# A hybrid encoder layer on one core: each recurrent head's four weight tiles as two units of seven products of block sums

## The chip, the cores and the metric

The kernel runs on one core of a Trainium2 chip. The metric is the time of one execution on the device in microseconds (us); three executions of the kernel before took 2068.74, 2071.32 and 2077.0 us, median 2071.32.

## The reference, cut to what matters

One layer over 1056 tokens (1024 of a prompt, 32 of a sample): a fused input projection, window attention (branch A), a gated linear recurrence (branch B), gates, an output projection and a convolutional FFN. The change is in branch B and in how its columns of the projection are multiplied:

```
h = _rms_norm(x, g_pre_mix);  z = h @ w_in            # 1024 x 7424 weights
qb, fb, ib, ob = the columns of z for branch B         # 8 heads x 128 columns each
f = lb + (1 - lb) * sigmoid(fb);  k = 1 - f;  q = silu(qb);  v = ib
cum = cumsum(log f) in blocks of 64 tokens
o = (q * exp(cum)) @ state + causal(q * exp(cum - mid) @ (k * exp(mid - cum)).T) @ v
state = exp(last) * state + (k * exp(last - cum)).T @ v
yb = rms_norm(o) * silu(ob)
```

All of it is float32. TensorE gets every operand as two parts, a rounded one (hi) and the rest (lo), so one product of a 128x128 weight block is three matmuls: hi x hi, hi x lo, lo x hi.

## The kernel before, in words

Tokens lie along the free axis in three column groups, `GR` (384, 384 and 288 wide; the last holds 256 prompt tokens and the sample). `La[g][k]` and `Lb[g][k]` are the hi and lo parts of h for row block k of group g; they stay in SBUF from the first stage until branch B is done. A weight tile is 1024x128, loaded by `load_raw`, split by `load_next` (ACT rounds, L174; DVE takes the rest, L177) and used as a `unit` of three blocks, one per group; a block is 24 matmuls (8 row blocks x 3, L193 to L195) into one PSUM bank of three (`mm`), in two halves of 12. `stream` runs the blocks and hangs small pieces of work behind each half.

The order of the stages: norm and transposes of x; attention, with the gate columns and q columns as filler (up to 390 us); the eight heads of branch B (390 to 890 us); four gate units (GB[4..7]); the products with w_br_a, w_br_b and w_out; the FFN's up projection (1240 to 1695 us, `up_unit`), which already multiplies by block sums; the down projection and the end.

A head of branch B is four units in the order i, og, f, q. `decay` (L723) takes the logarithm of f and scans it, `factors` (L733) makes the exponentials of a group, `k_turn` and `v_turn` transpose, `tile_in` (L797) and `tile_out` (L837) carry the recurrence over nine token tiles with the PSUM banks `s` (two) and `o` (one), `group_out` (L865) transposes a group of normalised outputs and gates them. A head's recurrence runs behind the units of the next head, one tile per two halves. Each engine executes its instructions in the order that the scheduler wrote down; where one waits, all behind it on that engine wait.

## Time and profile before

| What | Value |
|---|---|
| median of three runs | 2071.32 us |
| the profiled execution | 2065.69 us, its span 2064.0 us |
| TensorE busy | 2021.0 us (98%) |
| VectorE (DVE) busy | 1339.9 us (65%) |
| ScalarE (ACT) busy | 895.1 us (43%) |
| GpSimd (POOL) busy | 187.2 us (9%) |
| TensorE's granted clock in the head stage | 1.00 of full |

Busy is the union of an engine's instructions. Matmuls are pipelined: one starts before the one ahead of it has ended, so what a matmul costs TensorE is the step from its start to the next start, not its duration. The same holds in a small way on DVE and ACT.

### The profile page before, as it was taken

What the parts mean: (1) busy time and instruction counts of PE and PEld (TensorE: products, weight loads), DVE (VectorE), ACT (ScalarE), POOL (GpSimd) and SP (SyncE); (2) the same over time, 40 slices, a digit from 0 to 9 for tenths busy, and PEclk for the clock granted to TensorE, in tenths of its full rate; (3) what the DMA queues carried; (4) which work ended last, traced back from release to release, by engine and by line L of the source; (5) the groups of instructions that cost most, each with busy time, mean ns of one, the idle gap of its engine ahead of it and who ended that gap; (6) DMA issues with size and microseconds to landing.
All of it is one profiled execution on the core that took longest, in us unless ns stands there. A gap on an engine that the chain in (4) does not pass through costs nothing.

```text
span 2064.0 us, 37303 instructions
## 1 busy us (share of the span) xinstructions
PE 2021.0 (98%) x14474; PEld 1993.4 (97%) x14474; DVE 1339.9 (65%) x3070; ACT 895.1 (43%) x1984; POOL 187.2 (9%) x244
## 2 busy tenths in 40 slices
PE   7999999999999999999999989999999999999998
PEld 6999999999999999999999988999999999999998
DVE  6776778446665556654354678888888884655552
ACT  6554555444444444442123664333333344543432
POOL 1000000000000000000000012323333310000000
PEclk9999999999999999999999999999999999999999
DMA  7312221211111111267554463222222245654542
GB/s 228 104 60 76 79 65 62 70 42 56 43 42 54 55 41 56 64 200 236 164 177 126 130 196 99 71 94 70 86 73 83 73 137 189 222 179 168 166 132 81
DMA packets 253574, 224.34 MB, mean 109 GB/s; under 512 B 12421, under 2 KB 229016, under 8 KB 253397
## 3 DMA queue, kind: packets, MB, share of 16 engines
q1 hardware_dynamic: 251893, 217.48, 33.5%
q0 software_dynamic: 1504, 4.47, 0.7%
q8 instruction: 114, 1.87, 0.4%
q14 instruction: 63, 0.52, 0.1%
HBM read 167.07 MB, written 54.83 MB: 108 GB/s over the span
## 4 chain that ended last, share of the span: by engine, by line
PE 82%; DVE 8%; DMA 5%; ACT 2%; issue 2%; SPq 0%; POOL 0%; ACTq 0%; DVEq 0%; POOLq 0%
PE mm L193 18%; PE mm L195 17%; PE mm L194 17%; PE st L1284 6%; PE st L1282 6%; PE st L1283 6%; PE tr L450 1%; DVE wl L177 1%; PE s L816 1%; PE o L472 1%; DVE cb L731 1%; PE s L423 1%; DMA ac<-act_d 1%; PE o L473 1%; PE s L424 1%
## 5 line engine op out<-in xcount | busy, mean ns | idle before, releaser
L193 PE MATMUL mm<-La,wh 128*128 128x384 f32 (+1 forms) x1368 | 459.1, 336 | 0.0
L194 PE MATMUL mm<-Lb,wh 128*128 128x384 f32 (+1 forms) x1368 | 440.5, 322 | 0.0
L195 PE MATMUL mm<-La,wl 128*128 128x384 f32 (+1 forms) x1368 | 440.2, 322 | 0.0
L1282 PE MATMUL st<-op,wt 128*128 128x264 f32 x1232 | 349.4, 284 | 6.0 <-ACT Sp L1293 2.8
L1284 PE MATMUL st<-op,wt 128*128 128x264 f32 x1232 | 350.2, 284 | 0.0
L1283 PE MATMUL st<-op,wt 128*128 128x264 f32 x1232 | 348.2, 283 | 0.0
L177 DVE TENSOR_TENSOR wl<-wr,wh 128x1024 fp32r<-128x1024 f32 x166 | 202.9, 1222 | 163.5 <-ACT wh L174 156.3
L174 ACT CAST wh<-wr 128x1024 fp32r<-128x1024 f32 x145 | 152.0, 1049 | 266.7 <-PE mm L194 215.9
L193 PEld LDWEIGHTS mm<-La,wh 128*128 128x128 f32 x1368 | 257.3, 188 | 2.3 <-issue 1.6
L194 PEld LDWEIGHTS mm<-Lb,wh 128*128 128x128 f32 x1368 | 257.8, 188 | 0.0
L195 PEld LDWEIGHTS mm<-La,wl 128*128 128x128 f32 x1368 | 257.2, 188 | 0.0
L1282 PEld LDWEIGHTS st<-op,wt 128*128 128x128 f32 x1232 | 231.9, 188 | 7.2 <-ACT Sp L1293 3.0
L1283 PEld LDWEIGHTS st<-op,wt 128*128 128x128 f32 x1232 | 232.1, 188 | 0.0
L1284 PEld LDWEIGHTS st<-op,wt 128*128 128x128 f32 x1232 | 231.3, 188 | 0.1
L193 PE MATMUL mm<-ac,wh 128*128 128x352 f32 x528 | 170.8, 323 | 1.3 <-DVE Sp L1311 1.3
L195 PE MATMUL mm<-ac,wl 128*128 128x352 f32 x528 | 170.1, 322 | 0.0
L194 PE MATMUL mm<-ac,wh 128*128 128x352 f32 x528 | 169.5, 321 | 0.0
L1179 ACT CAST wt<-wu 128x512 fp32r<-128x512 f32 x132 | 81.5, 620 | 198.9 <-POOL ab L1268 99.8
L193 PE MATMUL mm<-Ra,wh 128*128 128x264 f32 x512 | 146.5, 286 | 4.7 <-DVE ta L955 3.4
L194 PE MATMUL mm<-Rb,wh 128*128 128x264 f32 x512 | 145.8, 285 | 0.0
L195 PE MATMUL mm<-Ra,wl 128*128 128x264 f32 x512 | 145.7, 285 | 0.0
L1180 DVE TENSOR_TENSOR wt<-wu,wt 128x512 fp32r<-128x512 f32 x132 | 108.3, 820 | 44.2 <-ACT wt L1179 44.0
(349 smaller groups left out, 4146.3 us busy)
## 6 DMA issues: line engine op xcount, KB each, us to landing
wr<-in_w_down_dram SPq DMA_DIRECT2D x66, 512.0 KB
wr<-in_w_in_dram SPq DMA_DIRECT2D x58, 512.0 KB
wu<-in_w_up_dram SPq DMA_DIRECT2D x44, 512.0 KB
act_d<-Up SPq DMA_DIRECT2D x22, 528.0 KB
ac<-act_d SPq DMA_DIRECT2D x66, 176.0 KB
wr<-in_w_out_dram SPq DMA_DIRECT2D x16, 512.0 KB
ya_d<-ya SPq DMA_DIRECT2D x8, 528.0 KB
ld<-ya_d SPq DMA_DIRECT2D x32, 132.0 KB
```

What stands on the lines that cost most here:

```text
L174: S.copy(hi[:], raw[:])
L177: V.tensor_tensor(lo[:], raw[:], hi[:].bitcast(F32), op=ALU.subtract)
L193: E.matmul(ps, wh, a, start=first and n == 0, stop=False)
L194: E.matmul(ps, wh, b, start=False, stop=False)
L195: E.matmul(ps, wl, a, start=False, stop=last and n == len(ks) - 1)
L423: E.matmul(o, q[:, c:c + P], K1[kv][:, k0:k0 + nk], start=True, stop=False)
L424: E.matmul(o, q[:, c:c + P], K2[kv][:, k0:k0 + nk], start=False, stop=True)
L1179: S.copy(t[:, 0], src)
L1180: V.tensor_tensor(t[:, 1], src, t[:, 0].bitcast(F32), op=ALU.subtract)
L1282: E.matmul(o, wh, xh, start=first and k == 0, stop=False, skip_group_check=True)
L1283: E.matmul(o, wh, xl, start=False, stop=False, skip_group_check=True)
L1284: E.matmul(o, wl, xh, start=False, stop=k == 3, skip_group_check=True)
```

## The change

For each head the tiles q and f form one unit, i and og another (`BU`). With the four 512-row quarters a11, a12 (of the first tile) and a21, a22 (of the second) and four blocks of h (rows 0 to 3 and 4 to 7 of groups 0 and 1), a unit computes the two output tiles for groups 0 and 1 from seven products of sums instead of eight products; group 2 is multiplied plainly, with the quarters a11, a12, a21 and a22, which are operands 0, 2, 5 and 6 of the eight that a unit prepares. A product is 12 matmuls, a "piece"; a unit is 11 pieces: 7 of 384 columns into the PSUM banks X, Y and Z, and 4 of 288 into G. The sums of h are made once: its float32 form goes to DRAM (`h_d`), GpSimd adds there in four steps during attention (`h_sums`), and the parts `TH`, `TL` are loaded before the heads. The sums of the weights are made on GpSimd per unit (`b_parts`), and ACT and DVE split eight operands of 512 columns per unit. Evictions (e0 to e10) combine the banks. The block La[1][0:4], Lb[1][0:4] is given up to hold `tf` and `cb` and is read back for the gate units (`back`). Further: the gate unit GB[3] runs alone between attention and the heads; the sums for the norm are taken for six tiles at a time and the scaling (`S.mul`) is on ACT; the affine map of f moves from DVE to ACT; the scan is in three parts; the PSUM bank `s` is single; the recurrence follows at one tile per one and a half pieces.

```diff
-    for h in range(8):
-        plan += [in_cols(c + h * P) for c in (3328, 4352, 2304, 1280)]
+    plan.append(GB[3])
+    n_first = len(plan)
     plan += GB[4:]
...
+        def h_sums(k):
+            top, low = (aq.tile([P, 768], F32, tag=f"hs{a}", name=nm("hs")) for a in range(2))
+            dma(top[:], h_d[:, k, :])
+            dma(low[:], h_d[:, k + 4, :])
+            b11, b12, b21, b22 = top[:, 0:384], top[:, 384:768], low[:, 0:384], low[:, 384:768]
+            G.tensor_tensor(b11, b11, b12, op=ALU.subtract)
+            G.tensor_tensor(b12, b12, b22, op=ALU.subtract)
+            G.tensor_tensor(b22, b22, b11, op=ALU.add)
+            G.tensor_tensor(b21, b21, b22, op=ALU.subtract)
+            for j, b in enumerate((b22, b12, b11, b21)):
+                dma(t_d[j][:, k, :], b)
...
+    SX = {0: (La[0][0:4], Lb[0][0:4]), 1: (rows4(TH[0]), rows4(TL[0])),
+          2: (La[0][4:8], Lb[0][4:8]), 3: (rows4(TH[1]), rows4(TL[1])),
+          4: (rows4(TH[2]), rows4(TL[2])), 6: (rows4(TH[3]), rows4(TL[3])),
+          7: (La[1][4:8], Lb[1][4:8])}
+    BU = []
+    for h in range(8):
+        BU += [(1280 + h * P, 2304 + h * P), (3328 + h * P, 4352 + h * P)]
...
+        def parts(src):
+            t = wp.tile([P, 2, 4, P], F32R, tag="wb", name=nm("wt"), bufs=8)
+            S.copy(t[:, 0], src)
+            V.tensor_tensor(t[:, 1], src, t[:, 0].bitcast(F32), op=ALU.subtract)
+            ready_b.append(t)
+        parts(a11)
+        G.tensor_tensor(s1, a21, a22, op=ALU.add)
+        G.tensor_tensor(s3, a11, a21, op=ALU.add)
+        G.tensor_tensor(a11, a11, s1, op=ALU.add)
+        yield
+        parts(a11)
+        yield
+        parts(a12)
+        G.tensor_tensor(a12, a12, a11, op=ALU.add)
+        yield
+        for src in (s3, s1, a21, a22, a12):
+            parts(src)
+            yield
...
     def s_bank():
-        return bank(pp, "s", 2)
+        return bank(pb, "s", 1)
...
+            return [(st("X", 0, True), e0), (g1a, None), (st("Y", 1, True), e2),
+                    (st("X", 2), lambda: f1(0, b("X"))), (cl("G", 2), lambda: f1(2, b("G", 288))),
+                    (st("Y", 3), e5), (st("Z", 4, True), e6), (g2a, None), (st("Y", 6), e8),
+                    (cl("G", 6), lambda: f2(2, b("G", 288))), (st("Z", 7), e10)]
...
-            V.tensor_scalar(tf[:], tf[:], mc1[:, h:h + 1], c1[:, h:h + 1], op0=ALU.mult, op1=ALU.add)
-            V.tensor_tensor_scan(cb[:], resets[:], bb[:], 0.0, op0=ALU.mult, op1=ALU.add)
+            for o, n in GR:
+                V.tensor_tensor_scan(cb[:, o:o + n], resets[:, :n], cb[:, o:o + n], 0.0,
+                                     op0=ALU.mult, op1=ALU.add)
+            S.activation(tf[:], tf[:], AF.Identity, scale=mc1[:, h:h + 1], bias=c1[:, h:h + 1])
...
+                    S.mul(os_, os_, rs[:m_, a:a + 1])
...
+            pieces += qf_unit(h) + io_unit(h)
+            at(m0 + 11, decay, h)
+            for g in range(3):
+                at(m0 + 12 + 3 * g, factors, h, g)
+            at(m0 + 14, k_turn, h, 0)
...
+            at(m1, v_turn, h, 1)
...
+                t_in = m1 + 1 + (j * 5 // 4 if last else j * 3 // 2)
```

In the order of a middle head, first TensorE where a group of outputs is transposed (`tr` is the transposes' bank, `ident` the identity, `mm` a block's bank). Before:

```order
L194 MATMUL mm_7202<-Lb_165,wh_6826 128x288
L195 MATMUL mm_7202<-La_159,wl_6827 128x288
L871 MATMUL tr_7265<-ident,os_6965 128x128 x3
L193 MATMUL mm_7278<-La_157,wh_6948 128x384
L194 MATMUL mm_7278<-Lb_160,wh_6948 128x384
```

Now, in the fourth piece of the i/og unit (`X` and `G` are its banks, `wt` a split operand, L1063 the outputs' transposes, L981 `k_turn`):

```order
L1063 MATMUL tr_7434<-ident,vk_7036 128x128
L815 MATMUL X_7334<-Lb_169,wt_7279 128x384
L1063 MATMUL tr_7434<-ident,vk_7036 128x128
L816 MATMUL X_7334<-La_163,wt_7279 128x384
L1063 MATMUL tr_7434<-ident,vk_7036 128x128
L981 MATMUL tr_7473<-ident,ke_7395 128x128 x3
L813 MATMUL G_7367<-La_167,wt_7279 128x288
```

The transposes of two groups, which wait for the scaling on ACT, now stand between the matmuls of one piece, and `k_turn` of the current head follows at once; before, one group stood between two blocks.

ScalarE, at the og tanh (`sg`) of a head. Before (`os` are outputs, L719 `v_turn`):

```order
L854 COPY os_6965<-o_6968 128x128
L856 ACTIVATE sq_6971,ss_6966<-os_6965 128x128
L693 ACTIVATE sg_6856<-mm_6952 128x384
L719 COPY vk_6855<-tr_6995 128x256
L721 COPY vk_6855<-tr_6995 32x128
```

Now (`wu` is a raw weight tile that GpSimd has added into, `rs` the norm's factors):

```order
L911 COPY vk_7552<-tr_7553 128x384
L733 CAST wt_7640<-wu_7416 128x512
L898 ACTIVATE sg_7575<-x_1323_7550 128x384
L955 ACTIVATE qx_7612<-d_1335_7610 128x2x128
L957 ACTIVATE qx_7612<-d_1335_7610 128x32
L733 CAST wt_7675<-wu_7416 128x512
L1055 ACTIVATE vk_6959<-vk_6959,rs_7499 128x128 x2
```

The cast of the second operand of the next unit, which needs GpSimd's sum, now stands ahead of the tanh, of a group's exponentials and of the scaling of the outputs.

VectorE, after the factors of a head's first group. Before:

```order
L782 SCALAR_TENSOR_TENSOR tq_6858<-tq_6858,cb_7260 128x384
L813 TENSOR_TENSOR am_7365<-s_7363,cmask 32x32
L828 SCALAR_TENSOR_TENSOR S_7368<-S_7361,dec_6602,s_7363 128x128
L707 SCALAR_TENSOR_TENSOR tq_6858<-tq_6858,mm_7342 128x384
L756 TENSOR_TENSOR qx_7387<-cb_7260 128x3x64
```

Now (L834 is the eviction e2, L1064 the gating of a group of outputs):

```order
L973 SCALAR_TENSOR_TENSOR tq_7108<-tq_7108,cb 128x384
L734 TENSOR_TENSOR wt_7413<-sa_7202,wt_7413 128x512
L834 TENSOR_TENSOR vt_7432<-s1c_7350,Y_7412 128x384
L1064 SCALAR_TENSOR_TENSOR sg_6983<-tr_7380,ghh,sg_6983 128x384
L1004 TENSOR_TENSOR am_7450<-s_7448,cmask 32x32
L1019 SCALAR_TENSOR_TENSOR S_7453<-S_7446,dec_6687,s_7448 128x128
L1064 SCALAR_TENSOR_TENSOR sg_6901<-tr_7434,ghh,sg_6901 128x384
L734 TENSOR_TENSOR wt_7456<-wu_7069,wt_7456 128x512
L943 TENSOR_TENSOR cb<-cb 128x3x64
```

Between two groups' factors now stand the splits of operands, an eviction and the gating of two groups.

## Rows read from the trace of the kernel before

**Rows 1.** The page: busy time of each engine; GB/s moved in 40 slices.
```profile
PE 2021.0 (98%) x14474; PEld 1993.4 (97%) x14474; DVE 1339.9 (65%) x3070; ACT 895.1 (43%) x1984; POOL 187.2 (9%) x244
...
GB/s 228 104 60 76 79 65 62 70 42 56 43 42 54 55 41 56 64 200 236 164 177 126 130 196 99 71 94 70 86 73 83 73 137 189 222 179 168 166 132 81
```
**Rows 2.** Windows: attention, one head, one unit of the up projection.
```profile
core 0: us, PE busy (x) PEld busy (x) DVE busy (x) ACT busy (x) POOL busy (x), PEclk, DMA share, GB/s
...
300.00:320.00 20.00, 20.00 (x142) 19.59 (x141) 17.95 (x53) 12.22 (x36) 1.83 (x10) 1.00 0.17 52
...
603.30:661.70 58.40, 58.06 (x383) 56.80 (x382) 35.63 (x121) 26.64 (x71) 0.00 (x0) 1.00 0.15 45
...
1371.00:1391.30 20.30, 20.30 (x170) 20.30 (x170) 16.65 (x25) 6.99 (x10) 7.02 (x5) 1.00 0.25 78
```
**Rows 3.** Waits in 428.1:836.9: who for whom, us in total, times, longest.
```profile
DVE am L818 <- PE s L816: 119.1, 42, 4.0
...
PEld o L851 <- ACT tq L706: 3.3, 6, 0.6
PE o L851 <- DVE am L813: 2.1, 6, 0.3
```
**Rows 4.** The tile tf: the logarithm of each head.
```profile
L729 ACT ACTIVATE bb<-tf,c,c x8: 1268/1268/1271, 428.1 to 836.9; 128x1056 f32<-128x1056 f32 x8
```
**Rows 5.** Timeline of PE in a head: start, us, line, tile, shape.
```profile
490.62 0.29 PE L193 MATMUL mm<-La,wh 128*128 128x288 f32 x1
...
491.81 0.29 PE L193 MATMUL mm<-La,wh 128*128 128x288 f32 x1
...
498.00 0.33 PE L193 MATMUL mm<-La,wh 128*128 128x384 f32 x1
...
500.08 0.33 PE L193 MATMUL mm<-La,wh 128*128 128x384 f32 x1
```
**Rows 6.** Timeline of DVE in a head.
```profile
543.20 0.83 DVE L730 TENSOR_SCALAR tf<-tf,mc,c 128x1056 f32<-128x1056 f32 x1
543.95 2.35 DVE L731 TENSOR_TENSOR_SCAN cb<-resets,bb 128x1056 f32<-128x1056 bf16 x1
...
550.01 0.55 DVE L777 TENSOR_TENSOR d<-d,tf 128x384 f32<-128x384 f32 x1
550.48 0.55 DVE L778 TENSOR_TENSOR ke<-ke,tf 128x384 f32<-128x384 f32 x1
...
560.30 0.60 DVE L873 SCALAR_TENSOR_TENSOR yb<-tr,ghh,sg 128x384 f32<-128x384 f32 x1
560.83 1.20 DVE L177 TENSOR_TENSOR wl<-wr,wh 128x1024 fp32r<-128x1024 f32 x1
565.83 0.28 DVE L818 TENSOR_TENSOR am<-s,cmask 64x128 int32<-64x128 int32 x1 [3.80 <-PE s L816]
...
566.45 0.29 DVE L826 COPY S<-s 128x128 f32<-128x128 f32 x1
...
585.87 0.67 DVE L861 TENSOR_SCALAR os<-os,rs 128x128 f32<-128x128 f32 x3
```
**Rows 7.** Timeline of DVE in a unit of the up projection.
```profile
1383.73 1.45 DVE L1180 TENSOR_TENSOR wt<-wu,wt 128x512 fp32r<-128x512 f32 x1
...
1388.33 0.69 DVE L1180 TENSOR_TENSOR wt<-wu,wt 128x512 fp32r<-128x512 f32 x1
1388.94 1.25 DVE L1260 TENSOR_TENSOR Up<-Up,rbT 128x1056 f32<-128x1056 f32 x1
```
**Rows 8.** Timeline of POOL in the same unit.
```profile
1374.51 2.20 POOL L1186 TENSOR_TENSOR wu<-wu,wu 128x512 f32<-128x512 f32 x1
...
1383.34 1.29 POOL L1192 TENSOR_TENSOR wu<-wu 128x512 f32<-128x512 f32 x1 [4.33 <-DVE wt L1180]
```
**Rows 9.** Waits of ACT in 1300:1560 (12.8 units of the up projection).
```profile
ACT wt L1179 <- POOL ab L1268: 59.1, 12, 5.0
```
**Rows 10.** Groups of instructions by form: ACT's casts of the up projection.
```profile
L1179 ACT CAST wt<-wu 128x512 fp32r<-128x512 f32 x132 | 81.5, 620 | 198.9 <-POOL ab L1268 99.8 <-PE st L1284 67.6 <-DVE wt L1180 22.6
```

More of the change, by code (lines that the diff above doesn't have):

```diff
@@ L112, in layer_kernel @@
     xt_d = dp.tile([P, 8, T], F32, name="xt_d")
+    h_d = dp.tile([P, 8, 768], F32, name="h_d")
+    t_d = [dp.tile([P, 4, 384], F32, name=f"t_d{j}") for j in range(4)]
     x1_d = dp.tile([P, 8, T], F32, name="x1_d")
@@ L643, in layer_kernel @@
             blocks += unit(gate_out(ta_d[i]))
-            if i in (0, 2, 4, 7):
-                blocks += unit(gate_out(tb_d[(0, 2, 4, 7).index(i)]))
+            if i in GB_AT:
+                blocks += unit(gate_out(tb_d[GB_AT.index(i)]))
             if i < 7:
@@ L662, in layer_kernel @@
         hi_on[0] = "act"
+    bctx = ExitStack()
+    tp = bctx.enter_context(right("tp"))
+    TH, TL = [], []
+    for j in range(4):
+        TH.append(tp.tile([P, 4, 384], F32R, name=f"TH{j}"))
+        TL.append(tp.tile([P, 4, 384], F32R, name=f"TL{j}"))
+        dma(TL[j][:].bitcast(F32), t_d[j][:])
+        for k in (0, 2):
+            src = TL[j][:, k:k + 2, :].bitcast(F32)
+            S.copy(TH[j][:, k:k + 2, :], src)
+            V.tensor_tensor(TL[j][:, k:k + 2, :], src, TH[j][:, k:k + 2, :].bitcast(F32),
+                            op=ALU.subtract)
@@ new lines, in layer_kernel, with b_raw, b_parts @@
+    NB = len(BU)
+    raw_b, ready_b, gens_b, n_b = {}, [], {}, [0]
+    def b_raw(u):
+        raw_b[u] = []
+        for c in BU[u]:
+            t = wp.tile([P, KT, P], F32, tag="wb" if u % 2 else "wr", name=nm("wu"),
+                        bufs=8 if u % 2 else 2)
+            dma(t[:], in_cols(c)[0])
+            raw_b[u].append(t)
+    def b_parts(u):
+        f1, f2 = raw_b.pop(u)
+        ss = wp.tile([P, KT, P], F32, tag="wb", name=nm("sa"), bufs=8)
+        s1, s3 = ss[:, 0:4, :], ss[:, 4:8, :]
+        a11, a12, a21, a22 = f1[:, 0:4, :], f1[:, 4:8, :], f2[:, 0:4, :], f2[:, 4:8, :]
+        def parts(src):
[16 more added lines that the diff above has]
+            yield
@@ new lines, in b_prepare @@
+    def b_prepare(n):
+        while n_b[0] < min(n + 1, 8 * NB):
+            u, i = divmod(n_b[0], 8)
+            if i == 0:
+                if u not in raw_b:
+                    b_raw(u)
+                gens_b[u] = b_parts(u)
+            next(gens_b[u])
+            if i == 4 and u + 1 < NB:
+                b_raw(u + 1)
+            n_b[0] += 1
+    small = {0: [lambda: b_prepare(0)], 2: [lambda: b_prepare(1)], 4: [lambda: b_prepare(2)]}
+    stream(unit(gate_out(tb_d[3])), small)
+    pctx.close()
@@ L665, in layer_kernel, with mm_bank, tr_bank, s_bank @@
+    pctx = ExitStack()
+    pb = pctx.enter_context(tc.tile_pool(name="pb", bufs=1, space=PSUM, reuse_waits="tile"))
+    n_bank = [0]
+    def mm_bank():
+        n_bank[0] += 1
+        return bank(pb, "XYZG"[n_bank[0] % 4], 1)
+    def tr_bank():
+        return bank(pb, "tr", 2)
+    def s_bank():
+        return bank(pb, "s", 1)
+    def o_bank():
+        return bank(pb, "o", 1)
     with right("bp") as bp:
@@ L896, in layer_kernel @@
-        tail = [b for c in range(4, 8) for b in unit(gate_out(tb_d[c]))]
-        stream(blocks + tail[:8], small)
+                at(m0 + 12 + 3 * g, factors, h, g)
+            at(m0 + 14, k_turn, h, 0)
+            at(m0 + 17, k_turn, h, 1)
+            at(m0 + 16, v_turn, h, 0)
+            at(m0 + 18, v_turn, h, 2)
+            at(m1, v_turn, h, 1)
+            last = h == 7
+            for j in range(9):
+                t_in = m1 + 1 + (j * 5 // 4 if last else j * 3 // 2)
+                at(t_in, tile_in, h, j)
+                at(t_in + 2, tile_out, h, j)
+                if j == 2:
+                    at(t_in + 1, k_turn, h, 2)
+                if j == 5:
+                    at(t_in + 4, group_out, h, 0)
+                    at(t_in + 5, group_out, h, 1)
+                if j == 8:
+                    at(t_in + (3 if last else 4), group_out, h, 2)
@@ new lines, in back, with more @@
+        def back():
+            for part, t in (("La", La), ("Lb", Lb)):
+                t[1][0:4] = rows4(lp.tile([P, 4, 384], F32R, tag=f"{part}10", name=nm(part)))
+            for k in range(4):
+                src = Lb[1][k].bitcast(F32)
+                dma(src, h_d[:, k, 384:768])
+            for k in range(4):
+                split(La[1][k], Lb[1][k], Lb[1][k].bitcast(F32))
+        def more():
+            limit[0] = n_mix
+            load_next()
+        at(len(pieces) - 3, back)
@@ L900, in layer_kernel @@
+        at(len(pieces) - 2, more)
+        for m, (run, ev) in enumerate(pieces):
+            run()
+            if ev is not None:
+                ev()
+            for f in small.pop(m, ()):
+                f()
+        tail = []
+        for c in range(4, 8):
+            u = unit(gate_out(tb_d[c]))
+            tail += [u[0], u[2], u[1]]
+        stream(tail[:8], {m - len(pieces): f for m, f in small.items()})
+    bctx.close()
     rp = ctx.enter_context(right("rp"))
```

245 lines of the change are left out of this document (142 added, 103 removed).

## The prediction, made before the changed kernel ran

> **What bounds the kernel now.** I read the page first, then windows over the stages, then who waits for whom in the heads, then timelines of TensorE and DVE inside one head and inside one unit of the up projection, which already works with block sums. TensorE is busy for 98% of the span, so time goes where TensorE's work goes [rows 1]. Inside the heads it stands still for almost nothing: of 58.40 us in a middle head it is busy 58.06, and in seven heads its waits for DVE and ACT sum to 2.1 and 3.3 us [rows 2, 3]. DVE has room there on average, 35.6 of 58.4 us, and most of its idle time is a wait for TensorE's scores; ACT has 26.6, GpSimd nothing [rows 2, 3]. The logarithms of the first and the last head start 408.8 us apart, so a head is 408.8 / 7 = 58.40 us [rows 4].
>
> **What the change removes on TensorE.** Twelve steps of matmuls of 384 columns took 500.08 - 498.00 = 2.08 us, 0.173 each; nine of 288 columns took 1.19 us, 0.132 each [rows 5]. A head before has 4 tiles x 2 groups x 24 = 192 of the first and 96 of the second: 33.3 + 12.7 = 46.0 us. The other 12.4 us of the 58.4 are the recurrence's matmuls and the transposes, which stay. After it has 2 units x 7 pieces x 12 = 168 and 96: 29.1 + 12.7 = 41.8. So TensorE needs 54.2 us per head, 4.16 less, and 33.3 us less over eight heads. The granted clock is full in the head's window [rows 2] and TensorE stays dense, so I leave it there.
>
> **What it adds on DVE and ACT, in total.** Per head DVE gets 16 splits of 512 columns at a step of 0.61 us (1388.33 to 1388.94) [rows 7] for four of 1024 at 1.20 [rows 6]: +5.0. Ten combinations of banks come in, of 384 columns like the product at 550.01, which steps by 0.47 [rows 6]: +4.7. The affine map of f goes (0.75), the scaling of the outputs (0.67 per three, 2.0) and one of three rounds of small norm instructions (about 1) [rows 6]. That is 41.5 us of 54.2 before any quarrel with GpSimd, 77%. ACT gets 16 casts of 0.62 [rows 10] for four of about 1.05, the map, the nine scalings and two copies: about 36 us, 67%. On average both fit; a unit of the up projection has DVE at 16.65 of 20.3 us, 82%, and TensorE waits for nothing [rows 2].
>
> **Where the work stands.** It doesn't lie evenly. All of the scan and the three groups' factors fall into the i/og half of a head, after `decay`. Before, that stretch of DVE ran without a gap from 543.20 to 562.03, 18.8 us [rows 6], and nothing on TensorE waited behind it, since blocks have three banks and the transposes of k come a unit later. Now take out of it the map (0.75), the scaling (0.6), two combinations of q (0.94) and a 1024-wide split (1.2): 15.3 remain. Add eight splits (4.9), five evictions (2.35), three combinations of og (1.3), the gating of two more groups (1.1, at 0.53 a step), a round of small instructions (0.9) and one more tile's mask and state (565.83 to 566.74, 0.9) [rows 6, 7]: 26.8 us. TensorE's own work in that half is 7 x 2.08 + 4 x 1.58 + 6.2 of the small = 27.1.
>
> To that comes GpSimd, which makes four sums of 512 columns per unit. In the up projection one split took 1.45 us instead of 0.69 while a sum ran beside it; the sum ran from 1383.34 to 1384.63, and the split ended 0.55 after it [rows 7, 8]. Another sum took 2.20 instead of 1.29 [rows 8]: the loss falls on either engine. Per unit the loss on DVE lies between 0 (GpSimd always waits) and 4 x 1.29 = 5.2. I take 2.5, half. DVE's half is then 29.3 us against 27.1, and it decides by 2.2 us.
>
> The Trainium skill (SBUF — State Buffer, section "Who interferes with whom") says that a DVE instruction with two SBUF inputs and a GpSimd instruction that reads SBUF lock each other out, and that the later one is blocked until the first has finished. The split above agrees: it finished one undisturbed run's length after the sum. By that rule alone, with DVE always the later one, the loss would be the upper end, 5.2 us; that is the third case below.
>
> Why 2.2 us on DVE become a wait of TensorE: the pieces use single banks. Y is written in pieces 2, 5 and 8 of a unit, and between them only two pieces (3.7 to 4.2 us) cover the eviction, which stands in DVE's queue behind factors and splits, as the order shows. At the half's end `v_turn` of group 1 waits for eviction e10, and e10 stands behind everything else of the half. In the other half DVE has 41.5 + 5 - 29.3 = 17.2 us for TensorE's 27, catches up and hides nothing more. **Waits through ACT** come on top. In the up projection ACT stood 59.1 us in 12 waits, 4.9 each, at a cast that needs GpSimd's sum [rows 9]; nothing was late there, for only casts stand behind it. Here the tanh of og, a group's exponentials and the scaling of the outputs stand behind that cast, and TensorE's transposes of the outputs, now between the matmuls of a piece, wait for the scaling. Between 0 (the sum is early) and 4.9 I take 0.8, near the lower end, as DVE is late at the same place and the two waits mostly fall together. So 54.2 + 2.2 + 0.8 = 57.2 us per head, 1.2 less than before, 9.6 over eight.
>
> **Edges.** In attention GpSimd makes 16 sums of 384 columns, about 1 us each by width, 0 to 16 us on a DVE that is busy 17.95 of 20 us at the densest [rows 2]; little of it is late, as the early windows are thinner: 1. The sums' parts are 4 x 786 KB to load when attention's tiles come free. The unit GB[3] (48 x 0.173 + 24 x 0.132 = 11.5 us) and two pieces (3.7) cover the first; at some 200 GB/s, as the dense slices move [rows 1], all four take 15.7: 0 to 5, I take 1. In the last head the four splits of the gate weights (1.20 each) and of the reloaded block stand in DVE's queue ahead of the first tile's mask, the reload starts only when `cb` is done, and the single bank s holds TensorE: 0 to 8, I take 4. The stores of h and the scan in three parts I count at nothing: the first lie on a queue that nobody waits for, the second costs two start-ups. Edges: 6, between 0 and 15.
>
> **The sum.** Against the profiled execution's 2065.69 us: -9.6 + 6 = -3.6, 2062.1. The median of the runs shown is 5.6 above that execution, so as a median 2067.7: 2068.
>
> **The rivals.**
> *The waits are absorbed (faster).* DVE is at about 80%, as in the up projection where TensorE never waits with three banks and the same eviction chain [rows 2]. If DVE's lead from the light half carries it through, a head is 54.2 to 54.8: -33.3 + 6 = -27, 2044. Against it: in the up projection DVE's load is the same in every unit; here one half is full.
> *DVE and GpSimd bind the second half (slower).* DVE is always the later one: 26.8 + 5.2 = 32.0 us, and ACT's wait at the cast adds 1.5 that DVE spends idle: 33.5 against 27.1. The head is then 60.6, +2.2, and 17.6 + 6 = +24: 2095. It decides from the point where DVE's half exceeds TensorE's by more than the 4.16 us saved. For it: the split of 1.45 us and the 59.1 us of ACT [rows 7, 9]; against it the sum of 2.20, where GpSimd lost [rows 8].
> *The edges are dear.* The heads as forecast, but the edges cost 18: +8, 2080. Against it: attention shows hardly a wait of TensorE now.
> That fewer matmuls are issued is sure from the order; that they would not shorten TensorE's work would need a longer step between the pieces, and the rows on both sides of a change of bank keep their step [rows 5], so I give that no case of its own.
>
> **How the numbers follow.** What a measurement of this kernel tells from no change is about 0.5%, 10 us. Forecast 0.40, with a head of 56.4 to 58.0 and edges of 3 to 9: 2058 to 2077; a quarter of it (0.10) is faster by over 0.5%, 0.05 slower, 0.25 within. Absorbed 0.27, all faster. DVE and GpSimd 0.25, all slower. Dear edges 0.08, 0.02 within and 0.06 slower. Faster 0.37, within 0.27, slower 0.36. The range reaches through most of the second and third case: 2040 to 2097, with about 0.07 left out on either side.
>
> **What would show it.** In the trace after, the step of the matmuls stays at 0.173 us and a head has 264 of them. The distance of the logarithms is the test: 57.2 forecast, 54.5 if absorbed, 60.6 if bound. In the i/og half DVE should show hardly a gap, some splits of about 1.4 us, and TensorE should wait there at `v_turn` of group 1, at Y's pieces and at the outputs' transposes, in the q/f half for almost nothing. Wrong would be: waits of TensorE in the q/f half, casts that are late (a piece waiting for its weights), a wait of more than 8 us at the start of the heads, or attention longer than now.

## The result and the profile after

The changed kernel took 2082.39 us (median of five runs, 2077.66 to 2083.61), the kernel before 2070.11 (median of five); the ratio is 1.005 with a 95% interval of 1.0028 to 1.0072. The forecast was 2068 within 2040 to 2097: it named a small gain or no change, and the change costs half a per cent. The profiled execution took 2079.95 us, its span 2078.2.

The page's busy times, the answer to [rows 1]:

```profile
PE 2011.2 (97%) x14282; PEld 1971.7 (95%) x14282; DVE 1430.1 (69%) x3096; ACT 966.0 (46%) x2182; POOL 290.6 (14%) x323
```

TensorE has 192 matmuls fewer and is busy 9.8 us less, but the span is 14.2 us longer, so it stands still more. Where, is read from three kinds of rows: the last scores of attention, the logarithms of the heads, and the first product of the gated branches behind the heads. First the kernel before, then after (source view; the numbers behind the durations are the first and the last start):

```profile
L423 PE MATMUL s<-K,qa x72: 222/284/388, 70.1 to 370.9; 128*128 128x256 f32 x56, 128*128 128x128 f32 x8, 128*128 128x160 f32 x8
L193 PE MATMUL mm<-Ra,wh x512: 279/282/422, 909.8 to 1201.0; 128*128 128x264 f32 x171
```
```profile
L423 PE MATMUL s<-K,qa x72: 222/306/390, 77.5 to 369.6; 128*128 128x256 f32 x56, 128*128 128x128 f32 x8, 128*128 128x160 f32 x8
L193 PE MATMUL mm<-Ra,wh x512: 281/282/422, 926.8 to 1215.6; 128*128 128x264 f32 x171
L918 ACT ACTIVATE cb<-tf,c,c x8: 1268/1269/1272, 422.2 to 836.5; 128x1056 f32<-128x1056 f32 x8
```

One gate unit fewer lies ahead of attention's last scores: GB[3], 11.5 us by the steps of [rows 5], has moved to between attention and the heads. Without it, the start with attention went from 359.4 to 369.6 (+10.2). From there to the branches it went, GB[3] on both sides, from 550.4 to 557.2 (+6.8). The rest went from 1154.2 to 1151.4 (-2.8). The sum is 14.2. The logarithms are (836.5 - 422.2) / 7 = 59.19 us apart, against 58.40 [rows 4]. Both are means over seven distances, and in both the first is shorter, since no recurrence runs behind the units of head 0: before it is 54.33 and the other six 59.05 to 59.10; after it is 53.79 and the others 59.69 to 59.96, once 61.19 (starts of the logarithms in ACT's timeline, the first three of which follow). So a head behind the first grew by 1.0 us in the mean of six (59.08 to 60.08), although TensorE has by the forecast 4.16 us less to do in it.

```profile
422.23 1.27 ACT L918 ACTIVATE cb<-tf,c,c 128x1056 f32<-128x1056 f32 x1
...
476.02 1.27 ACT L918 ACTIVATE cb<-tf,c,c 128x1056 f32<-128x1056 f32 x1
...
535.96 1.27 ACT L918 ACTIVATE cb<-tf,c,c 128x1056 f32<-128x1056 f32 x1
```

Who waits for whom in the heads (waits of TensorE in 420:850, then of ACT in 500:840: total us, times, longest), the answers to [rows 3, 9]:

```profile
PE tr L1063 <- ACT vk L1055: 18.9, 13, 2.4
PE tr L909 <- DVE vt L850: 2.5, 1, 2.5
PE tr L981 <- DVE ke L969: 0.5, 1, 0.5
```
```profile
ACT wt L733 <- POOL wu L741: 49.8, 12, 5.1
```

TensorE stands 21.9 / 7 = 3.1 us in a head, nearly all of it at the transposes of the outputs, in two places: about 0.65 us at groups 0 and 1, and 2.4 us at group 2 (behind the first logarithm, where no outputs are due yet, 2.5 us at `v_turn` in its place). In the kernel before it stood about 0.3. 4.16 less of work and 2.8 more of stops would still be a gain of 1.3. TensorE's timeline around the longer stop shows the rest (start, us, instruction, idle time ahead of it):

```profile
557.54 0.34 PE L813 MATMUL Y<-TH,wt 128*128 128x384 f32 x1
...
559.10 0.33 PE L813 MATMUL Y<-TH,wt 128*128 128x384 f32 x1
559.28 0.34 PE L815 MATMUL Y<-TL,wt 128*128 128x384 f32 x1
562.00 0.47 PE L1063 MATMUL tr<-ident,vk 128*128 128x128 f32 x1 [2.38 <-ACT vk L1055]
...
563.88 0.44 PE L813 MATMUL G<-La,wt 128*128 128x288 f32 x1
564.12 0.44 PE L815 MATMUL G<-Lb,wt 128*128 128x288 f32 x1
...
565.63 0.29 PE L813 MATMUL G<-La,wt 128*128 128x288 f32 x1
565.76 0.29 PE L815 MATMUL G<-Lb,wt 128*128 128x288 f32 x1
```

Behind the stop the matmuls of 288 columns step by 0.24 us, and 1.5 us later by 0.13 again, as in [rows 5]. The windows of the head before it say why (after the counts: granted clock, DMA share, GB/s):

```profile
498.00:501.00 3.00, 1.68 (x10) 1.35 (x8) 3.00 (x11) 1.26 (x4) 1.29 (x1) 1.00 0.00 0
501.00:504.00 3.00, 1.93 (x13) 1.63 (x14) 2.99 (x9) 2.86 (x10) 0.85 (x1) 0.97 0.00 0
504.00:507.00 3.00, 3.00 (x14) 2.93 (x13) 3.00 (x10) 2.80 (x8) 0.44 (x1) 0.50 0.15 49
507.00:510.00 3.00, 3.00 (x18) 3.00 (x17) 2.20 (x5) 0.00 (x0) 0.00 (x0) 0.96 0.59 175
```

The granted clock is 0.50 in the third window, 1.2 in place of 2.4 GHz: TensorE is busy without a gap, and from 504.9 to 506.3 its matmuls of 288 columns step by 0.24 us in place of 0.13. In 420:850 there are seven stops of 2.4 to 2.5 us. Between 0.4 us ahead of the end of each of the seven and 1.7 us behind it the clock fell, for 3 to 7 us. Windows of 1 us over that stretch, each with 1 less its clock, sum to 13.7 us withheld. In the kernel before the clock is full in the heads [rows 2], and windows over its other heads show no fall either.

What the withheld clock cost in time is somewhat less. In runs below with the same code in the heads some stops had no fall behind them: there the first distance is 52.4 us and a steady one 58.4, 402.8 for all seven, against the 414.3 here. That makes 11.5 us for the seven falls. So the +6.8 from attention to the branches is 11.5 for the lower clock and -4.7 for the rest.

Why the scaling (L1055) is late stands in the timelines of GpSimd, DVE and ACT in that head, one fence each:

```profile
552.65 1.45 POOL L739 TENSOR_TENSOR sa<-wu 128x512 f32<-128x512 f32 x1 [21.29 <-DVE ss L1049]
554.06 1.69 POOL L740 TENSOR_TENSOR sa<-wu,wu 128x512 f32<-128x512 f32 x1
558.35 1.29 POOL L741 TENSOR_TENSOR wu<-wu,sa 128x512 f32<-128x512 f32 x1 [2.60 <-DVE rst L208]
```
```profile
552.50 0.15 DVE L1049 TENSOR_SCALAR ss<-ss 128x3 f32<-128x3 f32 x1
...
552.84 1.28 DVE L204 TENSOR_SCALAR rsb<-ss 128x3 int32<-128x3 int32 x1
554.04 0.54 DVE L969 TENSOR_TENSOR ke<-ke,tf 128x384 f32<-128x384 f32 x1
554.50 1.26 DVE L205 TENSOR_SCALAR rsb<-rsb 128x3 int32<-128x3 int32 x1
...
557.51 0.67 DVE L734 TENSOR_TENSOR wt<-wu,wt 128x512 fp32r<-128x512 f32 x1
...
558.64 1.01 DVE L209 TENSOR_TENSOR rst<-rst,ss 128x3 f32<-128x3 f32 x1
...
561.07 0.15 DVE L210 SCALAR_TENSOR_TENSOR rs<-rst,rs 128x3 f32<-128x3 f32 x1
```
```profile
554.06 0.48 ACT L911 COPY vk<-tr 128x384 f32<-128x384 f32 x1 [0.83 <-PE tr L909]
559.67 0.62 ACT L733 CAST wt<-wu 128x512 fp32r<-128x512 f32 x1 [5.12 <-POOL wu L741]
...
561.55 0.98 ACT L1055 ACTIVATE vk<-vk,rs 128x128 f32<-128x128 f32 x3
```

Two chains end together. On DVE the square root for the norm is a row of small instructions, spread one by one among splits and factors; three of them, which take 0.15 to 0.16 us in the run without sums below, lasted 1.28, 1.26 and 1.01, each until the sum that GpSimd was making had ended (554.10, 555.75, 559.64). In six heads of the trace these three lasted the same, within 0.01 us. The last of the row ended at 561.2. On ACT the cast of the next unit's second operand stood 5.12 us for GpSimd's third sum, which adds in place over the tile that DVE's split of 557.51 reads and began 0.2 us behind that split (its row names the small instruction that ended in between). Behind it stand the tanh, two exponentials and one more cast, and the scaling began at 561.55.

### The profile page after: what moved, and what is told of

It is laid out like the page before. It is cut to its first block, busy times and chain, and to the rows that moved or that the text cites. A ratio compares the mean times of both kernels' runs of the same rounds, so it can differ in the third digit from the quotient of the medians.

```text
span 2078.2 us, 37421 instructions
## 1 busy us (share of the span) xinstructions
PE 2011.2 (97%) x14282; PEld 1971.7 (95%) x14282; DVE 1430.1 (69%) x3096; ACT 966.0 (46%) x2182; POOL 290.6 (14%) x323
## 4 chain that ended last, share of the span: by engine, by line
PE 77%; DVE 12%; ACT 3%; DMA 3%; issue 2%; POOL 1%; SPq 0%; ACTq 0%; DVEq 0%; POOLq 0%
PE mm L193 12%; PE mm L194 12%; PE mm L195 12%; PE st L1513 6%; PE st L1512 6%; PE st L1511 6%; PE tr L450 1%; DVE wt L734 1%; PE G L815 1%; PE G L816 1%; PE G L813 1%; PE Y L816 1%; DVE cb L920 1%; PE s L1007 1%; PE Y L813 1%
## 5 line engine op out<-in xcount | busy, mean ns | idle before, releaser
L177 DVE TENSOR_TENSOR wl<-wr,wh 128x1024 fp32r<-128x1024 f32 x134 | 164.6, 1228 | 136.8 <-ACT wh L174 125.3
L174 ACT CAST wh<-wr 128x1024 fp32r<-128x1024 f32 x115 | 120.7, 1049 | 223.0 <-PE mm L194 166.3
L1408 ACT CAST wt<-wu 128x512 fp32r<-128x512 f32 x132 | 81.5, 620 | 199.8 <-POOL ab L1497 99.8
L193 PE MATMUL mm<-La,wh 128*128 128x384 f32 (+1 forms) x504 | 166.2, 332 | 1.2 <-ACT La L216 1.2
L194 PE MATMUL mm<-Lb,wh 128*128 128x384 f32 (+1 forms) x504 | 163.8, 325 | 0.9 <-DVE Lb L217 0.9
L195 PE MATMUL mm<-La,wl 128*128 128x384 f32 (+1 forms) x504 | 163.1, 324 | 0.0
L434 ACT ACTIVATE sc<-sc,st 128x257 f32<-128x257 f32 (+1 forms) x144 | 69.6, 485 | 87.0 <-DVE st L429 77.2
L733 ACT CAST wt<-wu 128x512 fp32r<-128x512 f32 x96 | 58.3, 616 | 103.1 <-POOL wu L741 58.0
L193 PEld LDWEIGHTS mm<-Ra,wh 128*128 128x128 f32 x512 | 97.1, 190 | 5.1 <-ACT gt L285 3.2
```

What stands on the lines that cost most here:

```text
L174: S.copy(hi[:], raw[:])
L177: V.tensor_tensor(lo[:], raw[:], hi[:].bitcast(F32), op=ALU.subtract)
L193: E.matmul(ps, wh, a, start=first and n == 0, stop=False)
L194: E.matmul(ps, wh, b, start=False, stop=False)
L195: E.matmul(ps, wl, a, start=False, stop=last and n == len(ks) - 1)
L434: S.activation(sc[:m_, h, b0:e_ + 1], sc[:m_, h, b0:e_ + 1], AF.Exp, bias=st[:m_, 0, h:h + 1], scale=-1.0, accum_out=st[:m_, 1, h:h + 1])
```

## The experiments

All times are medians. "Head" is the mean distance of the logarithms, as the expectations use it; a "steady" head is one of the six distances behind the first. Three chips were used, each with the kernel before: transposes later, the first try of products, no sums, and rows in place ran beside 2069.97; one sum out, v later, both moves with the rows in place, and all later beside 2069.63; the other four beside 2072.29. A ratio is to the kernel before on the same chip. Each run has a trace of one execution.

**Transposes later.** In `group_out`'s schedule:

```diff
-                    at(t_in + 4, group_out, h, 0)
-                    at(t_in + 5, group_out, h, 1)
+                    at(t_in + 5, group_out, h, 0)
+                    at(t_in + 6, group_out, h, 1)
-                    at(t_in + (3 if last else 4), group_out, h, 2)
+                    at(t_in + (3 if last else 7), group_out, h, 2)
```

> The transposes of the outputs are issued later: groups 0 and 1 one piece later, group 2 (the one that stood 2.4 us in each head) three pieces later; the last head's group 2 stays. Nothing else is changed. Theory A (the stop and the lower clock behind it): the scaling is done at 562.5 in the head looked at, the transposes now come after 565, so the stop of 2.38 us goes, most of the 0.65 too, and with the stop the stretch of half clock behind it. The distance of the logarithms falls from 59.19 to 54.2 to 55.0 us, the mean granted clock rises from 0.987 to about 0.995, the time falls by 8 x 4.5 = 36 us to about 2046. Rival B (DVE and GpSimd set the length of a head): the stop only moves, to the pieces of Y or to the transposes of k and v; the distance stays above 58 and the time above 2072.

2068.93 us, ratio to before 1.0000 (0.9988 to 1.0013); head 57.59. Neither theory: the stop of 2.4 us is gone, and another stands in its place, at `v_turn` of group 1 (waits in 420:850):

```profile
PE tr L909 <- DVE vt L850: 14.5, 7, 2.5
PE tr L1063 <- ACT vk L1055: 4.5, 7, 0.6
```

The stop that took its place is 2.0 us, hardly less than 2.4, and yet a head is 1.6 shorter: behind these seven stops the clock fell only twice. Five steady heads take 57.92 to 57.96 us, the one with a fall in it 59.45. This is the first sign that the clock is a cost of its own.

**Products in the stop, first try.** In `group_out`, ahead of the transposes of group 2:

```diff
+            if g == 2 and h < 7:
+                for _ in range(14):
+                    E.matmul(t[:, 0:384], La[0][0][:, 0:P], La[0][0], start=True, stop=True)
```

> Ahead of the transposes of group 2's outputs, in the heads 0 to 6, TensorE makes 14 extra products of 384 columns into the bank that the transposes then overwrite: 14 x 0.173 = 2.42 us of work in the place of the stop of 2.38 us. The output stays as it is. Theory A: the stop is filled, so no time is added, and the clock no longer falls behind it; the head gives back only what the lower clock cost, some 1.8 us: distance 57.2 to 57.6, granted clock 1.00 in the heads, time down by 7 x 1.8 = 12 us to about 2070. Rival B (the clock is only a companion, and DVE sets the head): the head stays at 59 although the clock is full, and the time does not move. Rival C (the products come on top of the stop): head 61.5, time up by 16 us.

2101.31 us, 1.015 (1.0129 to 1.017), head 60.69. Rival C by its number, but the experiment missed its aim: the scheduler put the products ahead of the stop (in the second head they end at 501.2, the stop at 504.7), and it stayed (2.5 us). It does not decide between A and B. The clock fell behind four of its seven stops, which the table below takes up.

**Products in the stop, second try.** The same products, and group 2 issued two pieces later, which puts both directly behind the sixth piece of Y:

```diff
-                    at(t_in + (3 if last else 4), group_out, h, 2)
+                    at(t_in + (3 if last else 6), group_out, h, 2)
```

> The changed kernel with 14 extra products of 384 columns directly behind the sixth piece of Y, where TensorE stood for 2.38 us in each head, and the transposes of output group 2 behind them (heads 0 to 6; the products go into the bank that the transposes overwrite, the output stays). In the run with extra products before this one they lay 3 us too early and the stop stayed. The work added, 14 x 0.173 = 2.42 us, is as long as the stop. Theory A (the lower clock behind the stop is a cost of its own): no stop of 2 us, clock full, head 54.2 + 2.4 + 0.65 + small = 57.3 to 57.6 us, that is 1.6 to 1.9 us less than the 59.19 of the changed kernel although 14 more products are made; time down by 7 x 1.8 = 12 us to about 2070. Rival B (DVE and ACT set the head, the clock only falls because TensorE waits anyway): the head stays at 59.0 to 59.3, the time at 2082.

Head 57.41, as theory A said. TensorE's timeline and the logarithms:

```profile
559.16 0.33 PE L816 MATMUL Y<-TH,wt 128*128 128x384 f32 x1
559.33 2.59 PE L1064 MATMUL tr<-La 128*128 128x384 f32 x14
561.76 0.56 PE L1066 MATMUL tr<-ident,vk 128*128 128x128 f32 x3
562.48 0.29 PE L815 MATMUL G<-Lb,wt 128*128 128x288 f32 x1
562.61 0.29 PE L816 MATMUL G<-La,wt 128*128 128x288 f32 x1
```
```profile
L918 ACT ACTIVATE cb<-tf,c,c x8: 1269/1270/1272, 424.3 to 826.2; 128x1056 f32<-128x1056 f32 x8
```

With 14 products more, 2.43 us of work that is thrown away, a head is 1.78 us shorter; no window of 1 us in 440:800 shows a clock below full, and G's products behind step by 0.13 from the second on. Steady heads take 58.21 to 58.25, against 59.7 to 61.2 with the stop. The price of the lower clock, apart from the stop's, is shown for the heads. The whole did not follow: 2081.37 us, 1.0037 (1.0024 to 1.0051), 2070 expected. In its profiled execution the way from attention to the branches is 9.1 us shorter than in the changed kernel (548.1 against 557.2), and the stages behind, which nothing here touches, are 6.8 longer (1158.2 against 1151.4); there, windows of 2 us give 15.8 us lost by the clock against 6.8. Over all fourteen profiled executions these stages took 1151.3 to 1158.2. What decides there stays open, and it blurs every time below by some us; heads are therefore compared by the logarithms. Whether the heads kept the full clock in the other six executions is not known: they have no trace, and their mean granted clock was 0.987 to 0.991, against 0.990 in the traced one.

**No sums on GpSimd.** In `b_parts`, with s1 and s3 set to a21 and a22:

```diff
-        G.tensor_tensor(s1, a21, a22, op=ALU.add)
-        G.tensor_tensor(s3, a11, a21, op=ALU.add)
-        G.tensor_tensor(a11, a11, s1, op=ALU.add)
...
-        G.tensor_tensor(a12, a12, a11, op=ALU.add)
```

> GpSimd makes no sums of weights in the heads: the eight operands of a unit are taken from the loaded tiles as they are, so the outputs of this branch are not the reference's; casts, splits and products stay in number and size. Theory A with its cause (GpSimd's sums block DVE's instructions and hold the cast on which ACT stands, so the outputs' scaling is late): no small DVE instruction takes 1.0 to 1.3 us any more, ACT doesn't stand 5 us at the cast, the stop at the outputs' transposes falls under 0.3 us and the head to 54.2 to 55.0 us; time about 2045. Rival B (DVE's own queue is too full even without GpSimd): the small instructions of the square root are still spread over the pieces, TensorE still stands 1 us or more, the head is 56.5 to 58.

2052.01 us, 0.9909 (0.9893 to 0.9924). The head, 54.86, is theory A's; the time is 7 us above it, and a stop of 0.8 us is left where it said under 0.3. TensorE's waits in the heads:

```profile
PE tr L1058 <- ACT vk L1050: 5.7, 7, 0.8
```

The same splits and evictions stand on DVE; only GpSimd is quiet (and the sums' tile is gone from the ring of eight; TensorE waited for no weights in either kernel). So DVE's own queue is not what sets a head: in this order of instructions GpSimd's sums are, through the two chains.

**One sum out.** In `b_parts`:

```diff
-        G.tensor_tensor(a11, a11, s1, op=ALU.add)
```

> The changed kernel without GpSimd's third sum of each unit (a11 + s1): the second product takes a11 as it is, so the output of this branch differs. The cast on which ACT stood 5.1 us has then nothing to wait for but the load; the first two sums stay, and with them their hold on the square root's small instructions (1.28 and 1.26 us in the place of 0.15). Theory A1 (ACT's stand at the cast makes the scaling late): the stop of 2.4 us goes wholly, the head is 54.3 to 55.3. Theory A2 (the square root's chain on DVE is late by itself, ended 561.2 in the head looked at, only 0.4 us ahead of the scaling): DVE gains one blocked instruction, 0.9 us, so the stop falls from 2.4 to 1.2 to 1.5 us; the clock then mostly holds; head 55.5 to 57.

2070.51 us, 1.0005 (0.9994 to 1.0015), head 56.70; the stop at group 2 is 1.45 us, and the clock fell once. Theory A2: ACT's stand at the cast explains less than half of the stop. The rest goes only with the first two sums, which still held two small instructions here (1.28 and 1.26 us). How it divides between the engines is not separated: the norm's factors were ready at 557.0, and ACT came to the scaling at 557.2.

**The next wait moved too.** As the run with the transposes later, and:

```diff
-            at(m1, v_turn, h, 1)
+            at(m1 + 2, v_turn, h, 1)
```

> As the run with the later transposes of the outputs, and the transposes of v's group 1 are issued two pieces later as well (the stop that came next, 2.1 us in each head: they wait for the eviction of the unit's last piece). Theory A: with both places out of the way nothing of TensorE's is late in a head; stops fall from 2.8 to under 0.8 us a head, the clock stays full, the distance of the logarithms falls from 57.59 to 54.3 to 55.0 us, the time from 2069 to about 2049. Rival B (DVE and GpSimd set the length of a head, the stop moves again): a third place shows up, at Y's or Z's pieces or at the masks, and the distance stays above 56.5, the time above 2060.

2059.97 us, 0.9951 (0.9936 to 0.9967), head 55.99, between the two theories. The clock is full in all heads, and a third stop appears, a short one, where bank G waits for DVE's gating of og:

```profile
PE G L813 <- DVE sg L899: 5.6, 7, 0.8
PE tr L1063 <- ACT vk L1055: 4.6, 7, 0.7
```

**The start.** In `h_part`, `h` is written in place over `xc`:

```diff
-                h = np_.tile([P, GMAX], F32, tag="h", name=nm("h"), bufs=2)
+                h = xc
```

with 12 buffers of xc in place of 10. In the changed kernel DVE's waits in 20:64 show `h` waiting for its own store:

```profile
DVE h L539 <- DMA h_d<-h: 3.1, 4, 1.2
```

> At the start the normed rows are written over the columns' own buffer (12 buffers in the place of 10 and 2), so the next row no longer waits until one of two buffers has been stored. The heads stay as they are. Theory A for the start (the 7.4 us by which attention starts later come from DVE standing 3.1 us for the stores of h, and from loads that wait behind these stores): the wait for the store goes, attention's first scores come at about 73 us in the place of 77.5, the time falls by 3 to 5 us. Rival (the stores' bytes fill the DMA engines, whoever waits): scores at 77, no change.

2073.21 us, 1.0018 (1.0005 to 1.003), head 58.97. The wait is gone. The first scores come at 61.7, too early to compare, since the order changed; attention ends at 364.5 in place of 369.6, 5.1 us earlier:

```profile
L423 PE MATMUL s<-K,qa x72: 222/306/388, 61.7 to 364.5; 128*128 128x256 f32 x56, 128*128 128x128 f32 x8, 128*128 128x160 f32 x8
```

This end has a spread of its own. In seven traces with the start as in the changed kernel it lies at 369.6 to 373.0 (mean 371.3), in five with the rows in place at 363.3 to 364.8 (mean 364.3). So the two buffers cost 5 us against the trace of the changed kernel, which is the earliest of its seven, and 7 between the means.

**Neither stores nor sums of h**, and **in place without the sums.** In the first the stores and the 16 sums are left out, in the second, which also has h in place, only the sums. In both:

```diff
-        dma(TL[j][:].bitcast(F32), t_d[j][:])
+        dma(TL[j][:].bitcast(F32), xt_d[:, 0:4, 0:384])
-                small.setdefault(lo_ + 4, []).append(lambda i=i: h_sums(i - 2))
```

> The changed kernel without the stores of h and without GpSimd's 16 sums in attention; the sums' parts and the reloaded block are taken from the columns stored for the residual instead, so the outputs of this branch differ. The heads stay. Attention of the kernel before ended at 370.9 us, which is 359.4 without the unit GB[3]; in the changed kernel it ended at 369.6. Theory A (stores and sums are the whole of the 10.2 us): it ends at 359 to 361, time 2072. Rival (the new order of the gate units costs part of it): it ends at 364 or later.

2075.3 us, 1.0013 (1.0001 to 1.0025), head 58.80. Attention ends at 361.2, 0.2 behind theory A's range: 8.4 of the 10.2 us are stores and sums. This run's row, and the next one's:

```profile
L423 PE MATMUL s<-K,qa x72: 222/306/388, 70.7 to 361.2; 128*128 128x256 f32 x56, 128*128 128x128 f32 x8, 128*128 128x160 f32 x8
```
```profile
L423 PE MATMUL s<-K,qa x72: 222/306/388, 61.9 to 364.8; 128*128 128x256 f32 x56, 128*128 128x128 f32 x8, 128*128 128x160 f32 x8
```

> The run with the normed rows in place, without GpSimd's 16 sums in attention: the stores of h stay, the sums' parts are loaded from the residual's columns, so the outputs of this branch differ. With the rows in place attention ended at 364.5 us. Theory A (the rest of the start's cost is GpSimd's hold on DVE in attention): it ends 4 to 5 us earlier, at 360. Rival (the rest is the 3 MB of stores among the loads at the start): it ends at 363.5 to 364.5.

2074.63 us, 1.001 (0.9997 to 1.0022), head 58.34. It ends at 364.8, no earlier than with the sums: the rival. GpSimd's sums in attention cost nothing that shows beside a spread of 1.5 us; the 3.6 us between this run and the one before it come with the 3 MB of stores (one trace each). Up to 1.7 of them can be the clock, which fell at 65 us here and nowhere in attention in the other.

**All together.** Both moves and the rows in place; then groups 0 and 1 two pieces later as well; then G's first piece behind Y's:

> The two moves (outputs' transposes and v's group 1 later) together with the normed rows written in place at the start. If heads and start are independent, the gains add: 4.4 us a head from the moves and 4 to 9 us from the start, 2038 to 2046, below both kernels. If the start's gain only hid a wait further on, it comes out as the run with the moves alone.

2053.47 us, 0.9924 (0.991 to 0.9938), head 55.99. The start gives 6.5 on top of the moves: independent.

```diff
-                    at(t_in + 5, group_out, h, 0)
-                    at(t_in + 6, group_out, h, 1)
+                    at(t_in + (5 if last else 7), group_out, h, 0)
+                    at(t_in + (6 if last else 8), group_out, h, 1)
```

> As the run before it in this list, and the transposes of output groups 0 and 1 two pieces later than there, where 0.65 us a head were still waited. Theory A: those 0.65 us go too, head 54.0 to 54.6, 8 x 0.6 = 5 us less: 2034 to 2042. Rival: the transposes now lie closer to the ones of k and v and share their two banks, so another wait takes their place and the time stays.

2053.0 us, 0.992 (0.9906 to 0.9934), head 55.93. Missed: the outputs' stop fell from 0.65 to 0.2 a head, and G's rose from 0.8 to 1.0.

```diff
-            return [(st("X", 0, True), e0), (g1a, None), (st("Y", 1, True), e2),
+            return [(st("X", 0, True), e0), (st("Y", 1, True), e2), (g1a, None),
```

> As the run with all transposes later and h in place, and in each unit the first piece of the third column group comes behind the first piece of Y in the place of ahead of it: its bank was the last one waited for (0.8 to 1.1 us a head, for DVE's gating of og). Theory A: TensorE then waits for nothing longer than 0.3 us, head 54.3 to 55.0, time 2043 to 2049. Rival B (DVE sets the head in the i/og half): the wait comes back at the next piece that needs DVE, head 55.8 to 56.1, time 2053.

2050.6 us, 0.9886 (0.987 to 0.9903), head 55.17, between the two theories. G's stop is gone, and shorter ones stand at `k_turn` (up to 1.0 us) and at the bank s (up to 0.7):

```profile
PE tr L981 <- DVE ke L969: 4.1, 8, 1.0
PE s L999 <- DVE S L1017: 2.1, 6, 0.7
```

This version beats both kernels, by 1.1% and (by the two ratios) 1.6%, with the same arithmetic as the changed one; only the order of three kinds of transposes and one piece, and one buffer, differ.

The steady heads of these kernels side by side (the two that are left out, both moves with the rows in place and all later, have no fall, and 56.9 and 56.8). The four in the first rows have the same code in the heads, and the same seven stops:

| Kernel | stops in a head | clock fell after | steady head, no fall | with a fall |
|---|---|---|---|---|
| changed | 2.4 + 0.65 | 7 of 7 | | 59.7 to 60.0, 61.2 |
| rows in place | 2.4 + 0.65 | 6 of 7 | | 59.7 to 59.9, 61.2 |
| neither stores nor sums of h | 2.4 + 0.65 | 5 of 7 | 58.4 | 59.7 to 60.0, 61.2 |
| in place without the sums | 2.4 + 0.65 | 3 of 7 | 58.4 | 59.7 to 60.0, 61.2 |
| transposes later | 2.0 + 0.64 | 2 of 7 | 57.9 | 59.5 |
| one sum out | 1.45 + 0.64 | 1 of 7 | 57.3 | 58.9 |
| products ahead of the stop | 2.46 + 0.65 (and 2.42 of products) | 4 of 7 | 60.8 | 62.2 to 62.4, 63.7 |
| products in the stop | (2.43) + 0.65 | none | 58.2 | |
| v later too | 0.8 + 0.65 | none | 56.9 | |
| G later | 0.9 in short ones | none | 55.8, 56.3 | |
| no sums on GpSimd | 0.8 | none | 55.7 | |

A fall costs 1.3 to 1.6 us, a long one 2.8 or 2.9. Without one, a steady head less its stops and the products is 55.1 to 55.4 us in each row from the third to that of v later (58.4 - 2.4 - 0.65, 57.9 - 2.0 - 0.64, and so on), and 54.9 in the last two: a stop costs its length, a fall comes on top, and they are two terms. In one execution, of the run in place without the sums, both cases lie next to each other (two equal stops on TensorE, and the windows from 1.5 us behind each, the clock again ahead of the last two numbers):

```profile
612.71 0.33 PE L1061 MATMUL tr<-ident,vk 128*128 128x128 f32 x1 [2.40 <-ACT vk L1053]
...
671.11 0.33 PE L1061 MATMUL tr<-ident,vk 128*128 128x128 f32 x1 [2.40 <-ACT vk L1053]
```
```profile
614.20:617.20 3.00, 3.00 (x23) 2.99 (x22) 3.00 (x9) 2.87 (x9) 0.88 (x1) 1.00 0.20 59
672.60:675.60 3.00, 3.00 (x15) 2.92 (x15) 3.00 (x9) 2.83 (x8) 0.87 (x1) 0.50 0.18 57
```

In 3 us behind the first stop 23 matmuls are at work on TensorE, behind the second 15, in the same order of instructions.

## Why the prediction was wrong

**TensorE's work, 4.16 us less a head: nearly right.** The step stayed as it was: the ten from 557.54 to 559.28 are 0.174 each. The 58.4 and the 54.2 were means with the short first distance in them. Steady heads were 59.1, of which TensorE stood about 0.3 [rows 3]; 58.8 - 4.16 = 54.6 was to be expected, and the table gives 54.9 to 55.4. The 0.3 to 0.8 between them is not accounted for.

**The stops, 2.2 + 0.8 = 3.0 us: right in size, 3.1, and in part by luck.** They lie in the i/og half as forecast, and at the outputs' transposes. Y's pieces never waited. `v_turn` of group 1 waited once only, because the stop ahead of it had covered it; taken away, it stood there for 2.0 us a head. Which chain was late was half right: the forecast took the wait through ACT as 0.8 and put the rest on DVE's evictions. In truth two chains ran into the scaling: DVE's small instructions under GpSimd's sums, and the cast. That DVE's half is 2.2 us longer than TensorE's did not hold: with all of DVE's work and GpSimd's sums in place, the run with G later has a head of 55.17 by the mean, 2.0 under the forecast.

**The failed step: "The granted clock is full in the head's window [rows 2] and TensorE stays dense, so I leave it there."** The same text forecast 3 us of stops a head, so TensorE would not stay dense, and the window read was one of the kernel before. With the clock full, the same code takes 58.4 us in a steady head, 0.7 less than the 59.1 before; the forecast had 1.2 less. With a fall it takes 59.7 to 61.2. From attention to the branches the forecast was -9.6 + 5 = -4.6; measured is -4.7 without the clock and 11.5 for it. (The -4.7 is that near because two errors cancel: the seven distances gave 6.0 in place of 8.4, and the edges there cost less than 5.) This one missing term turned the heads from a gain into a loss. It is not the whole miss: without it the change would have come out at +2.7 of the span, because of the start's 10.2 below; with the start as forecast and the clock as it was, at +5.0. Either miss alone was enough for a loss. The Trainium skill (TensorE: Matmul & The Clock Gate, section "HAM oscillation — how this bites in real kernels") counts half the length of such a stretch as lost time. The rows come out a little under that: the windows from 501 to 510 withhold 1.7 us, and a fall of that size costs 1.3 to 1.6.

**GpSimd on DVE, 2.5 us per unit: nearly right.** In the i/og half the three small instructions lost 1.13, 1.11 and 0.86 us, 3.1 together, within the bounds of 0 and 5.2; what the q/f half lost was not summed. The prediction cited the Trainium skill (SBUF — State Buffer, section "Who interferes with whom") for a DVE instruction with two SBUF inputs. L209 has two, and agrees: it began while a sum ran and ended with it, at 559.65. L204 and L205 read one tile, which the rule as cited does not name, and were held in the same way. All three ended within 0.02 us of the sum; the split of [rows 7] ended 0.55 behind its sum, which is less than its undisturbed 0.69 and not, as the prediction read it, the whole of it. What the rule did not give is the consequence: the victims were links of a chain on which TensorE waits.

**Edges, 6 us: more, and from other places.** Start and attention cost 10.2 (taken as 1); "attention longer than now" was one of the prediction's own signs of being wrong. "The stores of h … I count at nothing: the first lie on a queue that nobody waits for" was wrong: DVE waited for them through the two buffers of `h`, which cost 5 to 7 us, and some 3.6 more come with their bytes. GpSimd's sums in attention, the bound of 16, cost nothing that can be seen. The loads of the parts and the tail, taken as 5, cost some 2 by an estimate: outside the seven distances the stretch from attention to the branches grew by 1.3 (557.2 - 414.3 = 142.9 against 550.4 - 408.8 = 141.6), with the eighth head's saving in it, 0.7 at a full clock. Part of the 10.2 can be the clock again: up to the end of attention it withheld 5.1 us, in the kernel before 1.7. The untouched stages behind gave 2.8 back, which lies within the spread of these stages and is luck.

**The sum.** -9.6 + 6 became -4.7 (attention to branches) + 11.5 (the clock there) + 10.2 (start and attention) - 2.8 = 14.2 of the span. As a median the change costs 12.3. Of the rivals, the one that DVE and GpSimd bind the second half had the sign and not the mechanism: with all of that work in place and only the order changed, the run with G later has 55.17 by the mean, where that rival gave 60.6 and the kernel before had 58.40.

## What to carry to other kernels

A stop of TensorE has two prices, its length and the stretch of half clock that may follow; where a change shortens TensorE's work but adds stops, both go into the sum, and the order is worth changing until no single stop is long: in the heads here, stops of up to 1.1 us cost only their length. That does not hold everywhere in this kernel: at the start of attention, in four of the five traces with the rows in place, the clock fell (at 64 to 65 us) behind stops of 0.5 and 1.1 us. Take a wait away only with the next one in view: here three stood behind each other, and the first move alone exchanged one for another. A store from a ring of two buffers is a wait for whoever writes the ring next, even where nobody waits for its queue.

## What the hardware showed beside this

A stop of one length does not always lower the clock: the same seven stops of 2.4 to 2.5 us, in the same code, did so seven, six, five and three times in four executions, stops of 2.5 behind the products four times in seven, stops of 2.0 to 2.5 twice in seven, of 1.45 to 1.6 once in seven, and stops up to 1.1 us never in the heads. What decides is not settled here. A kernel with such stops can have a spread of its own: of the eleven executions in place without the sums the fastest took 2066.34 us at a mean granted clock of 0.993, the slowest 2081.36 at 0.986. A DVE instruction on three columns per partition, 0.15 us by itself, lasted up to 1.28 us, until the GpSimd sum that it met had ended.
